# Seven-product pairs in the token mixers of a two-layer encoder on one core

## The chip, the cores and the metric

The kernel runs on one core of one Trainium2 chip. The metric is the device time of one execution in microseconds (us); the times shown are of several executions. The engines of the core have names of their own in the profile: PE is TensorE (PEld its weight loads), DVE is VectorE, ACT is ScalarE, POOL is GpSimd, SP is SyncE, which issues most of the transfers.

## The reference

Two layers work on 256 tokens of 2048 features. Each has a token mixer, a memory attention beside it that reads from the same input projection and writes through the same output projection, and a feed-forward network (FFN). All is in f32.

```python
for l in range(DEPTH):                                   # DEPTH = 2
    h = rms_norm(x, g_mix[l])
    if l % 2 == 0:                                       # layer 0: gated MLP
        tok_in, q_mem = split(h @ w_in_a, [3072])        # u and v, 1536 columns each, and 512 of q_mem
        tok_out = chunked_spatial_gating(tok_in, ...)    # gelu(u) * (w_s mixed rms_norm(gelu(v)) + b)
    else:                                                # layer 1: grouped-query attention
        tok_in, q_mem = split(h @ w_in_b, [2560])        # q 1536, k 512, v 512 columns
        tok_out = gqa_axial_attention(tok_in, ...)       # 12 query heads on 4 key heads, rotary
    mem_out = memory_attention(q_mem, mem, ...)          # 4 heads, 256 memory tokens, w_mem_kv
    x = x + concat([tok_out, mem_out]) @ w_out[l]        # 2048 x 2048
    x = x + swiglu(rms_norm(x, g_ffn[l]), w_gate_up[l], w_down[l])   # 5632 wide
```

## The kernel before

Every product keeps f32 accuracy by splitting both factors into a high part, rounded to the matmul's format, and a low part. `matmul3` (lines 196 to 200) then issues three matmuls for one product of 128x128 activations by 128x512 weights: high by high, low by high, high by low. A weight block comes from memory as a tile `raw` of 1 MB (four tiles of that kind exist); ScalarE casts it to `whi` (line 254) and VectorE subtracts to get `wlo` (line 255). Three `whi` and three `wlo` tiles exist, so weights are prepared at most some two blocks ahead of TensorE.

A projection is made in one of two forms. `Linear` (258 to 291) makes 512 output columns for both token blocks of 128: it goes through the 16 blocks of 128 input features, four to a weight tile, and issues 32 products. It prepares its weights in halves of 128x1024. It accumulates in two PSUM banks, and four such banks (`acc`) exist, so that one Linear can run while the one before is read out.

`Pair` (310 to 413) makes two groups of 512 columns in one call. It goes through eight units `i` of two feature blocks; a unit is a 2x2 block product (two token blocks, two feature blocks, two column groups) of eight products. For units listed in `fast` it uses a recursion of the Strassen kind with seven products: VectorE makes sums of weights (`T`, lines 347 to 350), and sums of activations have been made earlier (`activation_sums`, 300 to 308, from whole activations). A fast unit needs more accumulators: a Pair takes the four `acc` banks (its accumulators 2, 3, 4 and 8) and, from its first fast unit to the end of its last, also the four banks `m` (accumulators 1, 5, 6 and 7), which all transposes and attention steps use otherwise. After the last fast unit `inner` (393 to 406) reads the four `m` banks into SBUF tiles, or adds them to the residual when an `into` is given; `outer` (408 to 413) adds the `acc` banks at the end. Before, only the FFN uses Pair: gate and up together, and the down projection in two calls.

The order of the work around this is written by hand with a queue. Each Linear half-tile and each half unit of a Pair is a tick. `later(n, f)` puts f at n ticks from now: transposes of finished parts, scores, probabilities and weighted sums of the attention, residual turns, activation sums. From this order the framework makes the order of instructions on each engine, by a simulated time line with the order of the program as priority; so an engine's order is fixed before the run, and an instruction that must wait holds up what stands behind it on its engine.

Tiles of 128x512 f32 for anything short-lived come from a pool `a`: 36 of them in a mixer (`MIX_TILES`), 26 in an FFN.

In layer 0 the mixer runs three Linears for v, one for q_mem, keys and values of the memory, three for u, and four for w_out. After each u group `turn_u` (647) transposes the gated u into `cat`, the input of w_out. In layer 1 it runs k, v, three q groups (each followed by an `attend`, 461 to 525, with waits for its four steps: queries, scores, turn, weigh), q_mem, memory keys, memory values, and four for w_out. `add_residual` (586 to 597) adds a w_out result to X and queues the turn that makes the normed input of the FFN.

Of the kernel before, what the change touches and what calls it, by code (L numbers as in the profile page):

```python
# [16 lines left out]
P = 128  # L17
# [4 lines left out]
TOK = 1536  # L22
# [17 lines left out]
class Parts:  # L40


    def __init__(self):
        self.ap, self.whole = {}, {}
# [4 lines left out]
    def get(self, kc, t):  # L49
        return self.ap[kc, t]  # L50


@with_exitstack
def encoder(ctx: ExitStack, tc: tile.TileContext, x, mem, g_mix, g_ffn, w_in_a, g_v_a, w_spatial, b_spatial,
# [165 lines left out]
    def gained(tp, t, j, g, parts, keep):  # L220
# [9 lines left out]
        parts.whole[j, t] = hi, lo  # L230
# [17 lines left out]
    def halves(raw, n, step=KC4):  # L248
# [7 lines left out]
        return [(hi[:, c, :], lo[:, c, :]) for c in range(n)]  # L256

# [51 lines left out]

    class Pair:  # L310
# [28 lines left out]
        def prepare(self, i):  # L339
# [5 lines left out]
            if i in self.fast:  # L345
                T = room["p"].tile([P, KC3, NB], F32, tag="T", name=nm("T"), bufs=2)
                nc.vector.tensor_tensor(raw[:, 0], raw[:, 0], raw[:, 1], ALU.add)  # L347
                nc.vector.tensor_tensor(T[:, 0], raw[:, 0], raw[:, 3], ALU.add)
                nc.vector.tensor_tensor(T[:, 1], T[:, 0], raw[:, 1], ALU.subtract)
                nc.vector.tensor_tensor(T[:, 2], T[:, 0], raw[:, 2], ALU.add)  # L350
                self.ready[i] = raw, T

# [14 lines left out]
        def seven(self, i, raw, T):  # L367
            t1, w00, w10, w11 = halves(raw, KC4)
            t2, t3, t4 = halves(T, KC3)
# [23 lines left out]
        def inner(self):  # L393

            b, o = self.bank, self.into
            e, v, f, y = [room["p"].tile([P, NB], F32, tag=f"e{i}", name=nm("e"), bufs=1) for i in range(4)]
# [64 lines left out]
    def attend(qn, waits, keys, values, kv_of, kc0, parts):  # L461
# [42 lines left out]
        def weigh(pr):  # L504
# [12 lines left out]
            for hh in range(2):  # L517
                for t in range(NT):
                    ts = slice(t * P, (t + 1) * P)
                    parts.put(kc0 + 2 * pr + hh, t, hi[:, hh, ts], lo[:, hh, ts])  # L520
# [65 lines left out]
    def add_residual(acc, j, norm, g, parts):  # L586
# [7 lines left out]
        for t in range(NT):  # L594
            if acc:
                nc.vector.tensor_tensor(X[t][j], acc[t], X[t][j], ALU.add)
            later(1 + t, lambda t=t: turn(t))

    def residual_turns(j, norm, g, parts):
        add_residual(None, j, norm, g, parts)  # L600
# [4 lines left out]
    for l in range(DEPTH):  # L605
        scope = ExitStack()
        room["p"] = scope.enter_context(tc.tile_pool(name=f"mix{l}", bufs=MIX_TILES, reuse_waits="tile"))
        cat = Parts()
        m = Memory(l)
        if l == 0:  # L610
# [36 lines left out]
            def turn_u(us, t, c):  # L647
                tp = misc()
                transpose4(us, tp)
                hi, lo = split(v4(tp), [P, 4, P])  # L650
                for i in range(4):
# [52 lines left out]
            for c in range(3):  # L704
                acc = linear(hT, w, c * NB)
                for t in range(NT):
# [3 lines left out]
                    later(1 + t, lambda u=u, t=t, c=c: turn_u(u, t, c))  # L710
        else:
# [4 lines left out]
            acc = linear(hT, w, TOK)  # L716
            kn = head_norm(acc, norm.r, ghead["k"], True)
# [5 lines left out]
            own["v"] = scaled(linear(hT, w, TOK + MEMW), norm.r)  # L723
            for c in range(3):
                acc = linear(hT, w, c * NB)
                attend(head_norm(acc, norm.r, ghead["q"], True), (7, 8, 11, 13), lambda: own["k"], lambda: own["v"],
                       lambda h, c=c: (4 * c + h) // 3, 4 * c, cat)
            m.attend(linear(hT, w, TOK + 2 * MEMW), norm.r, cat)
            m.keys()
# [4 lines left out]
        units = kd if l else [(12, KC4), (0, KC4), (4, KC4), (8, KC4)]  # L734
        for j in range(4):
            add_residual(linear(cat, w_out[l], j * NB, units), j, norm, gslice("ffn", l), hF)
# [4 lines left out]
        room["p"] = scope.enter_context(tc.tile_pool(name=f"ffn{l}", bufs=FFN_TILES, reuse_waits="tile"))  # L741
        sums = {}
        fast = (0, 1, 2)

        def feature_sums(i):
            j, c = i // 2, 2 * (i % 2)
            whole = []
            for t in range(NT):
                hi, lo = hF.whole[j, t]
                a = big(F32, [P, 2, P])  # L750
                nc.vector.tensor_tensor(a, hi[:, c:c + 2].bitcast(F32), lo[:, c:c + 2].bitcast(F32), ALU.add)
                whole.append(a)
            sums[i] = activation_sums(*whole)
# [6 lines left out]
        for chunk in (range(0, 4), range(4, 8), range(8, 11)):  # L760
# [17 lines left out]
            for f in chunk:  # L778
                order, some = ((3, 4, 5, 0, 6, 1, 7, 2), 2) if f == 0 else ((0, 3, 1, 4, 2, 5, 6, 7), 3)
# [68 lines left out]
```

## Time and profile before

| | us |
|---|---|
| median of 3 runs | 2045.35 (2045.31 to 2046.12) |
| the profiled execution | 2045.77 |
| its span, first to last instruction | 2044.0 |
| TensorE busy in the span | 2028.7 |
| VectorE busy | 1604.7 |
| ScalarE busy | 1095.1 |

The profile is of one execution. Its span is 1.8 us shorter than its time, and its time is 0.4 us above the median. Busy times of TensorE are those of overlapping matmuls taken together; how closely matmuls follow each other is read from their start times.

### The profile page before, as it was taken

To read this page: it belongs to the slowest core of one execution; us is meant where nothing else is said; L and a number is where in the kernel's file an instruction comes from. 1 tells how busy PE (TensorE), PEld (TensorE's weight loads), DVE (VectorE), ACT (ScalarE), POOL (GpSimd) and SP (SyncE) were. 2 spreads that over 40 slices of the span, in tenths; PEclk is the share of its full clock that TensorE was granted. 3 is DMA by queue.
4 is the path that set the end of the run, shared out by engine and by line. 5 is a ranking of instruction groups with operands and counts; after the bars stand their busy time and mean duration, and the time that the engine had idled before them with its cause. 6 is when DMAs were issued, how large, how long until landed. Compare 5 with 4: busy or idle time off the path is not lost.

```text
span 2044.0 us, 24691 instructions
## 1 busy us (share of the span) xinstructions
PE 2028.7 (99%) x9298; PEld 1679.5 (82%) x9298; DVE 1604.7 (79%) x1862; ACT 1095.1 (54%) x1389; POOL 49.1 (2%) x80
## 2 busy tenths in 40 slices
PE   8999999999999999999999999999999999999999
PEld 6888888888888888888888888888888888888887
DVE  5575557998888988887666876589979899798976
ACT  7765455455444554445556665555544455444552
POOL 2010000000000000000010100000000000000000
PEclk9999999999999999999999999999999999999999
DMA  9754554655656556566556434655666555665554
GB/s 330 249 177 159 187 187 148 227 168 203 208 190 220 169 201 208 200 215 209 188 190 212 157 124 142 206 179 172 205 206 211 200 176 195 206 216 196 181 197 138
DMA packets 202432, 396.08 MB, mean 194 GB/s; under 512 B 11068, under 2 KB 11432, under 8 KB 202312
## 3 DMA queue, kind: packets, MB, share of 16 engines
q1 hardware_dynamic: 198800, 385.79, 56.4%
q0 software_dynamic: 2048, 6.42, 1.0%
q10 hardware_dynamic: 1464, 2.28, 0.3%
q8 instruction: 73, 1.20, 0.2%
q14 instruction: 47, 0.39, 0.1%
HBM read 390.26 MB, written 4.19 MB: 193 GB/s over the span
## 4 chain that ended last, share of the span: by engine, by line
PE 94%; DVE 3%; DMA 1%; issue 1%; ACT 1%; SPq 0%; DVEq 0%; ACTq 0%
PE acc L200 27%; PE acc L198 27%; PE acc L199 27%; PE m L200 4%; PE m L198 4%; PE m L199 4%; PE m L204 2%; DVE wlo L255 1%; DMA raw<-in_w_gate_up 1%; ACT whi L254 0%; PE m L500 0%; DMA x<-in_x 0%; DMA raw<-in_w_down 0%; PE m L643 0%; DVE x L413 0%
## 5 line engine op out<-in xcount | busy, mean ns | idle before, releaser
L255 DVE TENSOR_TENSOR wlo<-raw,whi 128x2048 fp32r<-128x2048 f32 (+2 forms) x465 | 836.4, 1822 | 227.0 <-ACT whi L254 224.8
L254 ACT CAST whi<-raw 128x2048 fp32r<-128x2048 f32 (+2 forms) x465 | 700.9, 1539 | 584.6 <-PE acc L199 513.3
L198 PE MATMUL acc<-whi,h 128*128 128x512 f32 x1440 | 563.6, 392 | 0.8 <-ACT whi L254 0.8
L199 PE MATMUL acc<-whi,h 128*128 128x512 f32 x1440 | 562.6, 391 | 0.0
L200 PE MATMUL acc<-wlo,h 128*128 128x512 f32 x1440 | 523.8, 392 | 1.1 <-DVE wlo L255 1.1
L198 PE MATMUL acc<-whi,a 128*128 128x512 f32 x1062 | 415.4, 392 | 0.6 <-DVE a L431 0.6
L199 PE MATMUL acc<-whi,a 128*128 128x512 f32 x1062 | 414.9, 391 | 0.0
L200 PE MATMUL acc<-wlo,a 128*128 128x512 f32 x1062 | 398.8, 391 | 0.1
L200 PEld LDWEIGHTS acc<-wlo,h 128*128 128x128 f32 x1440 | 270.6, 188 | 56.9 <-DVE wlo L255 1.9
L198 PEld LDWEIGHTS acc<-whi,h 128*128 128x128 f32 x1440 | 270.7, 188 | 55.4 <-ACT whi L254 1.2
L199 PEld LDWEIGHTS acc<-whi,h 128*128 128x128 f32 x1440 | 270.6, 188 | 55.0
L200 PEld LDWEIGHTS acc<-wlo,a 128*128 128x128 f32 x1062 | 199.7, 188 | 41.5 <-DVE wlo L255 0.5
L198 PEld LDWEIGHTS acc<-whi,a 128*128 128x128 f32 x1062 | 199.9, 188 | 41.3 <-DVE a L431 0.8
L199 PEld LDWEIGHTS acc<-whi,a 128*128 128x128 f32 x1062 | 199.9, 188 | 40.5
L254 ACT CAST whi<-T 128x1536 fp32r<-128x1536 f32 x82 | 121.4, 1481 | 143.3 <-PE acc L199 104.1
L255 DVE TENSOR_TENSOR wlo<-T,whi 128x1536 fp32r<-128x1536 f32 x82 | 143.5, 1750 | 38.8 <-ACT whi L254 38.8
L198 PE MATMUL m<-whi,a 128*128 128x512 f32 x264 | 104.2, 395 | 0.7 <-ACT whi L254 0.7
L199 PE MATMUL m<-whi,a 128*128 128x512 f32 x264 | 102.8, 390 | 0.0
L347 DVE TENSOR_TENSOR raw<-raw 128x512 f32<-128x512 f32 x82 | 56.1, 684 | 56.4 <-DMA raw<-in_w_gate_up 54.3
L200 PE MATMUL m<-wlo,a 128*128 128x512 f32 x264 | 89.6, 389 | 0.0
L192 ACT CAST a<-m 128x512 fp32r<-128x512 f32 x80 | 46.3, 586 | 50.7 <-PE m L204 32.6
L193 DVE TENSOR_TENSOR a<-m,a 128x512 fp32r<-128x512 f32 x80 | 54.0, 683 | 17.5 <-ACT a L192 17.5
(126 smaller groups left out, 1469.0 us busy)
## 6 DMA issues: line engine op xcount, KB each, us to landing
raw<-in_w_gate_up SPq DMA_DIRECT2D x352, 512.0 KB, 4.7
raw<-in_w_down SPq DMA_DIRECT2D x176, 512.0 KB, 5.2
raw<-in_w_out SPq DMA_DIRECT2D x32, 1024.0 KB, 5.1
raw<-in_w_in_a SPq DMA_DIRECT2D x24, 1024.0 KB, 5.3
raw<-in_w_in_b SPq DMA_DIRECT2D x24, 1024.0 KB, 5.2
raw<-in_w_mem_kv SPq DMA_DIRECT2D x16, 1024.0 KB, 5.2
raw<-in_w_in_a SPq DMA_DIRECT2D x7, 512.0 KB, 6.1
x<-in_x SPq DMA_DIRECT2D x8, 256.0 KB, 5.7
```

Of the source, the lines that this page charges most:

```text
L192: nc.scalar.copy(hi, src)
L193: nc.vector.tensor_tensor(lo, src, hi.bitcast(F32), ALU.subtract)
L198: nc.tensor.matmul(out, lhsT=a[0], rhs=b[0], start=start, stop=False)
L199: nc.tensor.matmul(out, lhsT=a[1], rhs=b[0], start=False, stop=False)
L200: nc.tensor.matmul(out, lhsT=a[0], rhs=b[1], start=False, stop=stop)
L204: nc.tensor.transpose(dst[:, c * P:(c + 1) * P], src[:, c * P:(c + 1) * P], ident)
L254: nc.scalar.copy(hi[:, cut], raw[:, cut])
L255: nc.vector.tensor_tensor(lo[:, cut], raw[:, cut], hi[:, cut].bitcast(F32), ALU.subtract)
L347: nc.vector.tensor_tensor(raw[:, 0], raw[:, 0], raw[:, 1], ALU.add)
```

## The change

Twelve Linears become six Pairs. In layer 0 the first two u groups are one Pair with three fast units of eight; in layer 1 keys and values are one Pair with two; w_out of each layer is two Pairs with two fast units each, which add into X. The third u group, v, all q groups and the memory projections stay Linears. For the fast units `pair_sums` makes activation sums of `hT` (as `mix_sums`) and of `cat` (as `cat_sums`, used by both Pairs of a w_out). In a mixer a fast unit takes its T from three tiles of the pool `a` instead of one of 128x1536, and `halves_of` casts and subtracts them one by one. `inner` takes its four tiles from `a` there as well. The residual turns of two groups are queued after each w_out Pair. The order of units in the first FFN Pair changes, and in layer 1 the turns and weighted sums of the second and third query group are queued one and two ticks later.

```diff
@@ Parts, gained, split
+    def put_pair(self, i, t, hi, lo):
+        self.two[i, t] = hi, lo
...
+    def halves_of(blocks):
+        hi = wp.tile([P, KC4, NB], F32R, tag="whi", name=nm("whi"))
+        lo = wp.tile([P, KC4, NB], F32R, tag="wlo", name=nm("wlo"))
+        for c, b in enumerate(blocks):
+            nc.scalar.copy(hi[:, c], b)
+            nc.vector.tensor_tensor(lo[:, c], b, hi[:, c].bitcast(F32), ALU.subtract)
+        return [(hi[:, c, :], lo[:, c, :]) for c in range(len(blocks))]
...
+    def pair_sums(parts, i):
+        whole = []
+        for t in range(NT):
+            hi, lo = parts.two[i, t]
+            a = big(F32, [P, 2, P])
+            nc.vector.tensor_tensor(a, hi.bitcast(F32), lo.bitcast(F32), ALU.add)
+            whole.append(a)
+        return activation_sums(*whole)
@@ Pair.prepare
-                T = room["p"].tile([P, KC3, NB], F32, tag="T", name=nm("T"), bufs=2)
+                if room["T"]:
+                    T = room["p"].tile([P, KC3, NB], F32, tag="T", name=nm("T"), bufs=2)
+                    T = [T, *(T[:, c] for c in range(KC3))]
+                else:
+                    T = [None, *(big() for _ in range(KC3))]
@@ add_residual
-    def add_residual(acc, j, norm, g, parts):
+    def add_residual(wait, j, norm, g, parts):
...
         for t in range(NT):
-            if acc:
-                nc.vector.tensor_tensor(X[t][j], acc[t], X[t][j], ALU.add)
-            later(1 + t, lambda t=t: turn(t))
+            later(wait + 1 + t, lambda t=t: turn(t))
@@ layer 0
-            for c in range(3):
-                acc = linear(hT, w, c * NB)
+            def gated(acc, c, wait):
                 for t in range(NT):
...
+            for i in range(3):
+                later(1 + 2 * i, lambda i=i: mix_sum(i))
+            g = Pair(hT, mix_sums, w, 0, NB, (3, 4, 0, 5, 1, 6, 2, 7), (0, 1, 2))
+            g.run()
+            for c in range(2):
+                gated([g.out[t][c] for t in range(NT)], c, 1 + 2 * c)
+            for i in range(2):
+                later(5 + 2 * i, lambda i=i: cat_sum(i))
+            gated(linear(hT, w, 2 * NB), 2, 1)
@@ layer 1
-            acc = linear(hT, w, TOK)
-            kn = head_norm(acc, norm.r, ghead["k"], True)
+            for i in range(2):
+                later(2 + 2 * i, lambda i=i: mix_sum(i))
+            g = Pair(hT, mix_sums, w, TOK, TOK + MEMW, (2, 3, 4, 0, 5, 1, 6, 7), (0, 1))
+            g.run()
+            kn = head_norm([g.out[t][0] for t in range(NT)], norm.r, ghead["k"], True)
...
-            own["v"] = scaled(linear(hT, w, TOK + MEMW), norm.r)
+            own["v"] = scaled([g.out[t][1] for t in range(NT)], norm.r)
...
-                attend(head_norm(acc, norm.r, ghead["q"], True), (7, 8, 11, 13), lambda: own["k"], lambda: own["v"],
+                attend(head_norm(acc, norm.r, ghead["q"], True), (7, 8, 11 + c, 13 + c), lambda: own["k"], lambda: own["v"],
...
+            for i in range(2):
+                later(2 + 8 * i, lambda i=i: cat_sum(i))
             m.keys()
             m.values()
@@ w_out
-        units = kd if l else [(12, KC4), (0, KC4), (4, KC4), (8, KC4)]
-        for j in range(4):
-            add_residual(linear(cat, w_out[l], j * NB, units), j, norm, gslice("ffn", l), hF)
+        orders = ((2, 3, 0, 4, 1, 5, 6, 7), (2, 3, 0, 4, 1, 5, 6, 7)) if l else \
+            ((6, 0, 7, 1, 3, 2, 4, 5), (6, 7, 0, 3, 1, 2, 4, 5))
+        pairs = []
+        for jj in range(2):
+            into = [[X[t][2 * jj + n] for n in range(2)] for t in range(NT)]
+            fast = (0, 1)
+            pairs.append(Pair(cat, cat_sums, w_out[l], 2 * jj * NB, (2 * jj + 1) * NB, orders[jj], fast, into))
+        for jj, g in enumerate(pairs):
+            g.run(None if jj else pairs[1])
+            for n in range(2):
+                add_residual(2 * n, 2 * jj + n, norm, gslice("ffn", l), hF)
@@ FFN, first Pair
-                order, some = ((3, 4, 5, 0, 6, 1, 7, 2), 2) if f == 0 else ((0, 3, 1, 4, 2, 5, 6, 7), 3)
+                order, some = ((2, 3, 4, 0, 5, 1, 6, 7), 2) if f == 0 else ((0, 3, 1, 4, 2, 5, 6, 7), 3)
```

49 lines of the change are left out of this document (26 added, 23 removed).

## The prediction

> **What bounds the kernel now.** I read the page first: busy shares, slices, the chain that ended last.
>
> ```profile
> span 2044.0 us, 24691 instructions
> PE 2028.7 (99%) x9298; PEld 1679.5 (82%) x9298; DVE 1604.7 (79%) x1862; ACT 1095.1 (54%) x1389; POOL 49.1 (2%) x80
> ...
> PE   8999999999999999999999999999999999999999
> ...
> DVE  5575557998888988887666876589979899798976
> ...
> PE 94%; DVE 3%; DMA 1%; issue 1%; ACT 1%; SPq 0%; DVEq 0%; ACTq 0%
> ```
>
> TensorE is busy almost everywhere and carries 94% of the chain; it is idle for 2044.0 - 2028.7 = 15.3 us in all. VectorE has room in the mixers (slices of 5 to 7) and little in the FFNs (8 and 9). Since busy matmuls overlap, I next took a gap-free stretch of the timeline of TensorE. Columns are start, duration, engine, line.
>
> ```profile
> 1263.24 0.40 PE L198 MATMUL acc<-whi,a 128*128 128x512 f32 x1
> ...
> 1277.33 0.39 PE L200 MATMUL acc<-wlo,a 128*128 128x512 f32 x1
> ```
>
> These are the first and the last of 63 matmuls in a row: 14.09 / 62 = 0.2273 us from start to start. Where TensorE never waits, that is the price of one. The windows then show where it waits (stretch, length, busy time and count for PE, PEld, DVE, ACT, POOL, then clock, DMA share, GB/s).
>
> ```profile
> 0.00:20.00 20.00, 14.43 (x65) 10.90 (x66) 10.76 (x24) 16.39 (x52) 2.42 (x10) 1.00 0.89 301
> 340.00:360.00 20.00, 18.86 (x83) 15.27 (x82) 16.76 (x20) 11.68 (x10) 0.00 (x0) 1.00 0.40 129
> 360.00:380.00 20.00, 19.69 (x85) 15.61 (x84) 20.00 (x22) 9.92 (x8) 0.00 (x0) 1.00 0.61 206
> 1200.00:1220.00 20.00, 16.79 (x88) 14.14 (x87) 13.02 (x35) 11.91 (x40) 1.83 (x2) 0.91 0.31 105
> 406.00:448.00 42.00, 42.00 (x191) 34.79 (x190) 38.01 (x40) 23.14 (x20) 0.00 (x0) 1.00 0.57 190
> ```
>
> Idle are 5.6 us at the start, which the change doesn't touch, 1.4 at the start of the first FFN, and 3.2 near 1206 in the mixer of layer 1. The last row is one FFN Pair with three fast units: VectorE busy for 38.0 of 42 us (90%), TensorE never idle. So a Pair with that load on VectorE runs without gaps.
>
> **The products.** A fast unit has seven products for eight, so it saves three matmuls. Fast units in mixers: 3 (u) + 2 (keys and values) + 4 Pairs of w_out x 2 = 13; the first FFN Pair keeps its two. 13 x 3 = 39 matmuls, and 39 x 0.2273 = **8.9 us**. Transposes and attention matmuls stay as many.
>
> The Trainium skill (Perfetto Trace Analysis, Identifying the Most-Contended Engine) says that matmul busy time is no measure of how near TensorE is to its limit, and that the busy share of its weight loads is one. By that this TensorE has 18% of headroom, and the 39 would be worth 0.82 x 8.9 = 7.3 us. The page here has weight loads at 82%, but in the gap-free FFN Pair above they are at 34.79 of 42, or 83%, so that share is already full; I keep 8.9, and the other figure lies inside my range.
>
> **What VectorE gets.** Rows by form (count, then busy us and mean ns):
>
> ```profile
> L255 DVE TENSOR_TENSOR wlo<-raw,whi 128x2048 fp32r<-128x2048 f32 x264 | 599.4, 2285 | 105.7 <-ACT whi L254 104.9
> L255 DVE TENSOR_TENSOR wlo<-raw,whi 128x1024 fp32r<-128x1024 f32 x199 | 235.6, 1220 | 119.2 <-ACT whi L254 117.9 <-PE m L204 0.7
> L255 DVE TENSOR_TENSOR wlo<-raw,whi 128x512 fp32r<-128x512 f32 x2 | 1.4, 692 | 2.0 <-ACT whi L254 2.0
> L348 DVE TENSOR_TENSOR T<-raw 128x512 f32<-128x512 f32 x82 | 56.0, 683 | 0.5
> L398 DVE TENSOR_TENSOR e<-m,e 128x512 f32<-128x512 f32 x32 | 21.8, 682 | 0.0
> L193 DVE TENSOR_TENSOR a<-a,a 128x512 fp32r<-128x512 f32 x15 | 10.2, 681 | 0.0
> L751 DVE TENSOR_TENSOR a<-h,h 128x256 f32<-128x256 f32 x12 | 4.5, 416 | 0.0
> L303 DVE TENSOR_TENSOR a<-a 128x128 f32<-128x128 f32 x15 | 4.2, 281 | 0.0
> L596 DVE TENSOR_TENSOR x<-acc,x 128x512 f32<-128x512 f32 x16 | 11.1, 692 | 15.3 <-PE acc L200 15.2
> L431 DVE SCALAR_TENSOR_TENSOR a<-acc,s,a 128x128 f32<-128x128 f32 x64 | 17.6, 342 | 0.0
> ```
>
> A fast unit adds four weight sums and three separate subtractions: 4 x 0.683 + 3 x 0.692 = 4.8 us. One activation sum costs 2 x 0.416 + 4 x 0.281 + 0.681 = 2.6 us; there are nine. `inner` is 4 x 0.682 = 2.7 us, adding into X as much again, and so is `outer`, which in w_out takes the place of as many additions (L596, 0.692). A weight tile in one piece saves 2 x 1.220 - 2.285 = 0.15 us. Whether that has cover is seen by stage:
>
> ```profile
> 114.00:139.00 25.00, 25.00 (x140) 21.64 (x139) 18.11 (x31) 14.56 (x39) 3.17 (x5) 1.00 0.44 140
> 139.00:162.00 23.00, 23.00 (x120) 19.47 (x119) 16.48 (x35) 13.93 (x28) 1.06 (x1) 1.00 0.52 180
> 162.00:184.00 22.00, 22.00 (x117) 18.72 (x116) 13.87 (x18) 11.88 (x17) 0.00 (x0) 1.00 0.45 144
> 184.00:207.00 23.00, 23.00 (x107) 19.05 (x106) 12.03 (x12) 10.46 (x12) 0.00 (x0) 1.00 0.54 183
> ...
> 230.00:252.50 22.50, 22.50 (x105) 18.64 (x104) 12.03 (x12) 10.32 (x12) 0.00 (x0) 1.00 0.55 188
> 252.50:275.00 22.50, 22.50 (x105) 18.64 (x104) 13.27 (x18) 12.41 (x24) 0.00 (x0) 1.00 0.55 188
> 275.00:298.00 23.00, 23.00 (x107) 19.02 (x107) 13.30 (x19) 12.36 (x24) 0.00 (x0) 1.00 0.55 183
> 298.00:320.50 22.50, 22.50 (x105) 18.64 (x104) 13.60 (x17) 12.16 (x22) 0.00 (x0) 1.00 0.54 179
> ...
> 1030.00:1052.00 22.00, 22.00 (x106) 18.31 (x105) 14.84 (x27) 14.45 (x34) 3.10 (x6) 1.00 0.57 187
> 1052.00:1074.00 22.00, 22.00 (x100) 18.22 (x100) 15.85 (x27) 12.12 (x26) 3.52 (x5) 1.00 0.68 218
> ```
>
> - w_out of layer 0 (230 to 320.5): VectorE 52.2 of 90.5 us. After: 52.2 - 16 x 0.15 + 4 x 4.8 + 2 x 2.7 + 2 x 2.7 = 79.8, on 90.5 - 12 x 0.227 = 87.8 us of TensorE: 91%, the load of the FFN Pair. Cost nothing; without that cover, each us that VectorE lacks is one of TensorE.
> - The u Pair (162 to 207): 25.9 of 45 becomes 25.9 - 8 x 0.15 + 3 x 4.8 + 2.7 + 2.7 + 3 x 2.6 = 52.3 on 43.0 us. Over by 9.3. Of that `outer` (2.7) falls after the last product, and two weight tiles (4.6) can be ready when the Pair begins, which leaves 2.0 us of idle TensorE.
> - Keys and values (1030 to 1074): 30.7 of 44 becomes 30.7 - 1.2 + 2 x 4.8 + 2.7 + 2.7 + 2 x 2.6 = 49.7 on 42.6. Over by 7.1; but again `outer` falls behind, and so does the norm of the keys (8 x 0.342 = 2.7 and its rotary steps), so about 0 is left.
>
> From below these two starts cost nothing, from above 9.3 + 7.1 = 16.4 us, if no tile is ready ahead. I take 2.0 and, for an order fixed ahead that doesn't quite fit, as much as the first FFN start shows (1.14 + 0.31): **+3.5**. At the two FFN starts the turns of two column groups come together, where one came before. That is eight more gain operations (0.34 as L431, nearest by size) and two more additions, 4.1 us of VectorE each, in front of the same three units of eight products; bounds -1.4 to +8.2 for both, taken as 0, since the first fast unit comes fourth there as before.
>
> ScalarE gets 39 casts for T, nothing longer than what VectorE does with them, at a share of 54%. PSUM: the four `m` banks are taken from the first to the last fast unit; by the lists of units the transposes and weighted sums due in a Pair come before that stretch, so I cost it at nothing; a read-out that is late would hold TensorE for about one subtraction, 0.68 us, at each of six Pairs. From a Linear to a Pair the last two `acc` banks must be read within half a unit, 12 x 0.227 = 2.7 us; two reads of the size of L596 take 1.4, so that costs nothing either while VectorE is on time. The transfers carry the same bytes in halves of 512 KB; their shares of time stay near 0.55. For SyncE's queue that is 48 more issues. What holds that queue is shown by its waits (us in total, times, longest):
>
> ```profile
> SPq L357 <- DVE wlo L255: 1037.5, 247, 11.6
> ```
>
> It stands waiting for VectorE to release a `raw` tile for half of the span, so its own time is covered; a late subtraction delays the next transfer too, which is part of the 16.4 above.
>
> **The later turns.** The gap near 1206:
>
> ```profile
> 1205.67 0.28 PE L200 MATMUL m<-a,a 128*128 128x256 f32 x1
> 1208.58 0.63 PE L500 MATMUL m<-ident,a 128*128 128x128 f32 x4 [2.63 <-DVE a L490]
> 1209.79 0.79 PE L198 MATMUL acc<-whi,a 128*128 128x512 f32 x1 [0.58 <-DVE a L431]
> ...
> 1213.22 0.39 PE L200 MATMUL acc<-wlo,a 128*128 128x512 f32 x1
> ```
>
> ```profile
> 1183.28 0.36 DVE L427 TENSOR_SCALAR s<-s,s 128x4 f32<-128x4 f32 x2 [0.73 <-POOL s L185]
> ...
> 1208.61 2.15 DVE L431 SCALAR_TENSOR_TENSOR a<-acc,s,a 128x128 f32<-128x128 f32 x8
> ```
>
> Transposes of probabilities (L500) stand first in TensorE's queue and wait 2.8 us for the softmax; then the memory values wait 0.8 for a bank; then eight matmuls take 3.43 us instead of 1.82, at a lower clock. Together 5.2 us. The turn moves back by two ticks of 12 matmuls (5.4 us), so its wait could go. But next in line is the bank: the values need the accumulators of q_mem, and L431, which reads those, came at 1208.61, though its factor was there at 1183.28. It lacked room: by my count the pool `a` then holds 16 memory tiles, 4 of own values, 2 of keys, 8 of `cat`, 1 of gains and 4 of turned queries, 35 of 36. The change adds an activation sum there (5 tiles while made, 2 kept). So the gap may go (-5.2) or come twice (+5.2). I take **-1.5**: its first wait shortens, its second stays. Behind a waiting transpose stands all of TensorE.
>
> **Sum.** -8.9 + 3.5 - 1.5 = -6.9 us. The profiled execution took 2045.77 (span 2044.0 and 1.8 around it), 0.4 above the median; from the median, 2045.35 - 6.9 = **2038.5 us**.
>
> **Rivals.** (1) As forecast, 2038.5: for it the FFN Pair without gaps; chance 0.50. (2) No new gap, and the old one goes: -8.9 - 5.2, **2031.3**. For it that most stretches have no idle time; against it the crowded starts; 0.18. (3) The pool `a` in layer 1 is the bound: the sums take tiles, q_mem's accumulators are held for longer, the gap comes twice: -8.9 + 3.5 + 5.2 = -0.2, **2045.2**, no change. For it the 25 us that L431 waited; 0.20. (4) Slower: VectorE becomes the bound at the starts of the u Pair and the key-value Pair, because the sums stand in its queue ahead of the weights and no tile is ready: +16.4 - 8.9 = +7.5, **2052.9**. It beats the gain from 8.9 us of new idle time on. For it 122% of load on paper; against it the FFN, and the slack of VectorE in the stage before (the first two rows of the stages, memory keys and values: 18.11 of 25 and 16.48 of 23 us, 72%); 0.12. That fewer matmuls are not issued can't be: the lists fix their number.
>
> **How the numbers follow.** This kernel's measurement tells 0.2% (4.1 us) from no change. Faster by that (under 2041.3): nearly all of (1), all of (2), 0.66. Within: (3) and a little of (1), 0.22. Slower (over 2049.4): (4), 0.12. The range runs from (2) to past (3), 2031 to 2047, and leaves out (4) and the outer ends.
>
> **What would show it.** Right: 39 fewer matmuls, idle time of TensorE of 14 to 20 us, idle pieces at the start of the u Pair, VectorE near 90% in w_out. Wrong: idle time over 24 us, or TensorE waiting for `wlo` through a whole Pair (4), or a gap of over 5 us beside memory keys or values (3). Under 13 us means (2).

## The result and the profile after

The changed kernel is slower: 2060.84 us median of four runs (2058.98 to 2062.43) beside 2045.73 (2045.31 to 2046.52) of the kernel before on the same chip, a ratio of 1.0074 with a 95% interval of 1.0062 to 1.0086. The forecast of 2038.5 us missed, by the sign too; the time lies outside the forecast range (2031 to 2047) and above the slowest rival (2052.9). The changed code is five lines further down: the weight cast and subtraction are L259 and L260, the matmuls L202 to L204, transposes L208, the norm of heads L460, the turns of probabilities L529. The page of the profiled execution (2058.98 us):

```profile
span 2057.2 us, 24904 instructions
PE 2028.7 (99%) x9259; PEld 1675.0 (81%) x9259; DVE 1700.2 (83%) x2016; ACT 1119.0 (54%) x1395; POOL 57.0 (3%) x80
...
DVE  5578889998889988887588877899979899798976
...
PE 92%; DVE 5%; ACT 1%; issue 1%; DMA 0%; SPq 0%; DVEq 0%; ACTq 0%
```

There are 39 matmuls fewer, as counted. TensorE is idle for 2057.2 - 2028.7 = 28.5 us, 13.2 more than before, just what the span gained, and over the 24 us that the prediction named as a sign of being wrong. That its busy time did not fall by 8.9 us is no contradiction: a matmul behind a long wait can take longer (0.63 us instead of 0.39 near 1217), and short waits vanish inside overlapping ones. So the busy total hid the loss, and the length of each stage shows it. The table takes the time from the first 128x512 product of a stage on TensorE's timeline to that of the next; "expected" is the saved products at 0.2273 us, and in the w_out and FFN rows the eight transposes (0.7 us; four in a row without a wait take 0.35 us from the first start to the next matmul's) of one column group that are now turned in the FFN's start instead of in w_out.

```
stage                               before   after    change   expected   lost
u (layer 0)                          71.96    77.72    +5.8      -2.0      7.8
w_out, layer 0                       90.82    89.43    -1.4      -3.4      2.0
FFN 0, first four gate-up Pairs     172.86   175.47    +2.6      +0.7      1.9
keys and values, q groups, q_mem    146.39   145.21    -1.2      -1.4      0.2
memory keys, values, w_out, layer 1 160.85   164.38    +3.5      -3.4      6.9
FFN 1, first four gate-up Pairs     171.43   175.56    +4.1      +0.7      3.4
```

The waits of TensorE (what waits, releaser: us in total, times, longest) name where:

```profile
PE m L529 <- DVE a L519: 4.4, 4, 1.3
...
PE m L208 <- DVE a L460: 3.2, 1, 3.2
PE m L202 <- ACT whi L268: 3.1, 1, 3.1
PE acc L202 <- ACT whi L259: 1.9, 3, 1.1
PE m L204 <- DVE wlo L260: 1.7, 2, 0.9
...
PE acc L202 <- DVE a L442: 1.4, 1, 1.4
PE acc L202 <- ACT a L744: 1.1, 1, 1.1
```

They are the softmax, the norm of heads, the cast of a sum of weights in the u Pair (L268), weights at the FFN starts, and two banks that are not yet read out. The windows of the stages shown before, in the same columns:

```profile
162.00:184.00 22.00, 22.00 (x118) 18.74 (x117) 19.93 (x36) 10.59 (x17) 0.00 (x0) 1.00 0.30 96
184.00:207.00 23.00, 18.82 (x76) 14.82 (x75) 18.51 (x27) 14.17 (x17) 0.00 (x0) 0.93 0.40 137
...
262.00:284.00 22.00, 22.00 (x100) 18.23 (x100) 19.10 (x19) 9.06 (x9) 0.00 (x0) 1.00 0.76 241
...
306.00:326.00 20.00, 20.00 (x90) 16.55 (x89) 20.00 (x20) 11.18 (x11) 0.00 (x0) 1.00 0.76 263
...
1200.00:1220.00 20.00, 16.84 (x89) 14.28 (x88) 13.98 (x34) 12.39 (x38) 1.83 (x2) 0.91 0.44 145
1250.00:1270.00 20.00, 15.64 (x87) 13.16 (x86) 14.50 (x34) 10.25 (x30) 0.00 (x0) 0.91 0.09 27
```

In the two windows of w_out Pairs (262 to 284, 306 to 326) TensorE has no gap, with VectorE at 87 and 100%. The loss lies in the seams: inside the u Pair, at 1211 (the old gap near 1206), and at 1255, where there was none. In the u Pair, the timeline of VectorE (start, duration, line; idle before in brackets) shows why:

```profile
186.24 0.75 DVE L330 TENSOR_TENSOR a<-h,h 128x256 f32<-128x256 f32 x2
187.02 0.29 DVE L317 TENSOR_TENSOR a<-a 128x128 f32<-128x128 f32 x1
...
188.78 0.69 DVE L197 TENSOR_TENSOR a<-a,a 128x512 fp32r<-128x512 f32 x1 [0.74 <-ACT a L196]
189.39 0.69 DVE L376 TENSOR_TENSOR a<-raw 128x512 f32<-128x512 f32 x1
190.11 0.69 DVE L377 TENSOR_TENSOR a<-a,raw 128x512 f32<-128x512 f32 x1
```

The activation sums of a later unit (L330, L317 to L320, L197) stand ahead of the weight sums (L376 to L378) that the next products need. TensorE started its last ready matmul at 187.37 and the next one, on the first of these sums, at 190.86.

### The profile page after: what moved, and what is told of

Read it like the earlier page. It is cut to its first block, busy times and chain, and to the rows that moved or that the text cites. A ratio compares the mean times of both kernels' runs of the same rounds, so it can differ in the third digit from the quotient of the medians.

```text
span 2057.2 us, 24904 instructions
## 1 busy us (share of the span) xinstructions
PE 2028.7 (99%) x9259; PEld 1675.0 (81%) x9259; DVE 1700.2 (83%) x2016; ACT 1119.0 (54%) x1395; POOL 57.0 (3%) x80
## 4 chain that ended last, share of the span: by engine, by line
PE 92%; DVE 5%; ACT 1%; issue 1%; DMA 0%; SPq 0%; DVEq 0%; ACTq 0%
PE acc L204 26%; PE acc L202 25%; PE acc L203 25%; PE m L204 4%; PE m L202 4%; PE m L203 4%; DVE wlo L260 2%; PE m L208 2%; ACT whi L259 1%; DVE a L197 0%; ACT a L514 0%; PE m L529 0%; DMA raw<-in_w_out 0%; PE m L678 0%; DVE x L442 0%
## 5 line engine op out<-in xcount | busy, mean ns | idle before, releaser
L259 ACT CAST whi<-raw 128x2048 fp32r<-128x2048 f32 (+2 forms) x417 | 695.8, 1694 | 582.1 <-PE acc L203 520.4
L260 DVE TENSOR_TENSOR wlo<-raw,whi 128x2048 fp32r<-128x2048 f32 (+2 forms) x417 | 833.3, 2017 | 172.6 <-ACT whi L259 171.4
L202 PE MATMUL acc<-whi,h 128*128 128x512 f32 x1410 | 552.9, 393 | 3.4 <-ACT whi L259 1.9
L203 PE MATMUL acc<-whi,h 128*128 128x512 f32 x1410 | 552.0, 391 | 0.0
L204 PE MATMUL acc<-wlo,h 128*128 128x512 f32 x1410 | 509.8, 392 | 0.4 <-DVE wlo L260 0.4
L202 PE MATMUL acc<-whi,a 128*128 128x512 f32 x1027 | 403.3, 393 | 1.1 <-ACT a L744 1.1
L203 PE MATMUL acc<-whi,a 128*128 128x512 f32 x1027 | 401.2, 391 | 0.0
L204 PE MATMUL acc<-wlo,a 128*128 128x512 f32 x1027 | 378.0, 391 | 0.2 <-DVE wlo L260 0.2
L202 PEld LDWEIGHTS acc<-whi,h 128*128 128x128 f32 x1410 | 265.7, 188 | 58.6 <-ACT whi L259 5.1
L204 PEld LDWEIGHTS acc<-wlo,h 128*128 128x128 f32 x1410 | 265.1, 188 | 55.8 <-DVE wlo L260 1.6
L203 PEld LDWEIGHTS acc<-whi,h 128*128 128x128 f32 x1410 | 265.6, 188 | 53.9
L204 PEld LDWEIGHTS acc<-wlo,a 128*128 128x128 f32 x1027 | 193.4, 188 | 41.6 <-DVE wlo L260 1.4
L202 PEld LDWEIGHTS acc<-whi,a 128*128 128x128 f32 x1027 | 193.6, 188 | 40.8 <-ACT a L744 1.6
L203 PEld LDWEIGHTS acc<-whi,a 128*128 128x128 f32 x1027 | 193.6, 188 | 39.2
L259 ACT CAST whi<-T 128x1536 fp32r<-128x1536 f32 x82 | 121.4, 1480 | 132.7 <-PE acc L203 95.1
L260 DVE TENSOR_TENSOR wlo<-T,whi 128x1536 fp32r<-128x1536 f32 x82 | 143.8, 1754 | 37.7 <-ACT whi L259 37.7
L202 PE MATMUL m<-whi,a 128*128 128x512 f32 x311 | 122.8, 395 | 3.8 <-ACT whi L268 3.1
L203 PE MATMUL m<-whi,a 128*128 128x512 f32 x311 | 121.2, 390 | 0.0
L375 DVE TENSOR_TENSOR raw<-raw 128x512 f32<-128x512 f32 x95 | 65.3, 687 | 58.7 <-DMA raw<-in_w_gate_up 47.8
L204 PE MATMUL m<-wlo,a 128*128 128x512 f32 x311 | 107.6, 390 | 1.7 <-DVE wlo L260 1.7
L202 PEld LDWEIGHTS m<-whi,a 128*128 128x128 f32 x311 | 58.4, 188 | 19.5 <-ACT whi L259 4.6
L204 PEld LDWEIGHTS m<-wlo,a 128*128 128x128 f32 x311 | 58.4, 188 | 14.7 <-DVE wlo L260 2.6
```

What stands on the lines that cost most here:

```text
L202: nc.tensor.matmul(out, lhsT=a[0], rhs=b[0], start=start, stop=False)
L203: nc.tensor.matmul(out, lhsT=a[1], rhs=b[0], start=False, stop=False)
L204: nc.tensor.matmul(out, lhsT=a[0], rhs=b[1], start=False, stop=stop)
L259: nc.scalar.copy(hi[:, cut], raw[:, cut])
L260: nc.vector.tensor_tensor(lo[:, cut], raw[:, cut], hi[:, cut].bitcast(F32), ALU.subtract)
```

## The experiments

All parts of the change sit behind constants in a copy of the changed kernel: `U_PAIR`, `KV_PAIR` and `OUT_PAIRS` choose Pair or the Linears of before, `LATER` the later turns (1 or 0), `FIRST` the unit order of the first FFN Pair. Lines are five further than in the changed kernel (L207 for L202), in the kernels with a staggered Pair twelve more. Medians are in us; the ratio is to before on the same chip, with its 95% interval.

```
only_u       2052.05  1.0036 [1.0024, 1.0049]   out_first    2044.14  0.9998 [0.9988, 1.0007]
only_kv      2044.27  0.9996 [0.9986, 1.0005]   out_stagger  2044.17  0.9994 [0.9984, 1.0004]
only_out     2048.86  1.0020 [1.0010, 1.0030]   all_parts    2048.63  1.0019 [1.0009, 1.0028]
only_turns   2045.49  1.0003 [0.9993, 1.0012]   qn_room      2039.84  0.9974 [0.9964, 0.9985]
u_early      2045.95  1.0005 [0.9995, 1.0015]   before_room  2040.20  0.9978 [0.9969, 0.9987]
u_stagger    2045.95  1.0003 [0.9994, 1.0013]   room_out     2042.47  0.9990 [0.9980, 0.9999]
out_late     2049.94  1.0024 [1.0014, 1.0033]   room_all     2044.58  0.9998 [0.9989, 1.0008]
out_room     2047.90  1.0014 [1.0005, 1.0024]   room_qTV     2042.33  0.9987 [0.9978, 0.9997]
room_t18     2053.32  1.0041 [1.0026, 1.0056]   room_qTV_u   2045.31  1.0000 [0.9991, 1.0010]
```

### One part at a time

`only_u`: the u Pair alone, the rest as before. The other three of this part differ from it by these constants only.

```diff
-KV_PAIR = True
-OUT_PAIRS = True
-LATER = 1
-FIRST = (2, 3, 4, 0, 5, 1, 6, 7)
+KV_PAIR = False
+OUT_PAIRS = False
+LATER = 0
+FIRST = (3, 4, 5, 0, 6, 1, 7, 2)
```

> The u Pair of layer 0 alone, the rest as before. Theory 1 (the loss of the u stage is made there: activation sums and T stand in VectorE's queue in front of weights, and the two hand-overs wait): the u stage takes 77.7 us where it took 72.0, so the kernel is some 5.8 us slower than before, about 2051.5 us, with a gap of about 3 us after the second fast unit begins and the lower clock behind it. Rival (the u stage suffers from the w_out Pairs behind it, whose T and sums are prepared in its last part): the stage is shorter than before by 9 x 0.227 = 2 us, about 2043.7 us. Layer 1 unchanged by both.

The u stage took 78.3 us and TensorE waited 3.1 us for the first weight sum at the same place: the loss of the u Pair is its own.

`only_kv`: `KV_PAIR = True` alone.

> Keys and values of layer 1 as one Pair alone. Theory 1: the stage had no loss after the change (145.2 us where 146.4 were), so -6 x 0.227 = -1.4 us, 2044.4 us, and the gap near 1206 stays at its 5 us. Rival (the Pair shifts the attention behind it and makes the two gaps of layer 1): 6 us of gaps more beside the memory keys and values, about 2050 us.

Its stage became 1.2 us shorter, nearly the six products. No loss.

`only_out`: `OUT_PAIRS = True` with the new `FIRST`.

> The four w_out Pairs alone, with the new order of the first FFN Pair, turns as before. Theory 2 (the two gaps of layer 1 come from the activation sums of w_out, which take tiles of the pool while the attention needs them): -24 x 0.227 = -5.5, +6 in the memory keys and values, +2 in w_out of layer 0, +5 at the two FFN starts: about +7.5, 2053 us. Rival (the gaps come from the later turns): without the 6, about +1.5, 2047 us, with the gap near 1206 as before.

w_out of layer 0 came out 3.5 us shorter, all that was expected. But the FFN starts grew by 2.6 and 3.9 us, and near 1250 TensorE lost 3.4 us around the softmax of the memory attention (4.8 us in which only sixteen transposes ran), where it had lost none. The 2.0 us lost in w_out of layer 0 in the full change come from its neighbour: with Linears for u it took 87.3 us in every run with w_out Pairs, with the u Pair 88.8 to 89.4.

`only_turns`: `LATER = 1` alone.

> Only the later turns and weighted sums of the second and third query group. Theory 2: the gap near 1206 stays or shrinks by its first wait, -2.8 to 0 us, 2043 to 2045.7 us. Rival (the later turns make the two gaps of layer 1): a second gap of some 6 us near 1255, about 2052 us.

```profile
PE m L213 <- DVE a L465: 3.1, 1, 3.1
```

The gap near 1206 stayed; only its releaser changed, from the softmax to the norm of the memory queries. The later turns gain nothing.

### Mending the u Pair and the FFN starts

`u_early`: `only_u` with the sums made during the three Linears before.

```diff
+            for i, n in enumerate((3, 12, 20)):
+                later(n, lambda i=i: mix_sum(i))
             m.attend(linear(hT, w, 2 * TOK), norm.r, cat)
...
-                for i in range(3):
-                    later(1 + 2 * i, lambda i=i: mix_sum(i))
```

> The u Pair alone (as in only_u), with its three activation sums made earlier: in the q_mem, the memory keys and the memory values, 3, 12 and 20 ticks after the last v group. Theory 1 (order in VectorE's queue: sums stand ahead of the weights of the second fast unit): the gap of 3.1 + 0.6 us near 190 and the low clock behind it go, the wait of 1.4 us where the third u group takes over the banks stays; u stage about 72 to 73 us, kernel about 2046 us. Rival (VectorE is short of time over the whole stage, whatever its order): gaps of about the same sum elsewhere in the stage, 2050 to 2052 us.

The wait for L273 is gone, and the u stage takes 73.7 us instead of 78.3. Twelve score matmuls of 128x256 have moved into it from the stage of the memory values, which became 1.5 us shorter (24.15 instead of 25.61). So the two stages are compared together: 97.8 us, after 103.9 in `only_u` and 97.6 with Linears. The sums where they stood were the cause. Whether it was their place or their load isn't separated, since the run also takes them out of the stage (VectorE busy for 58.7 us there, after 64.2); in `only_u` VectorE was busy for 64.2 of 78.3 us, so over the stage it had time left. But 1.8 us of waits came near 166, where the memory attention's softmax and its values' read-out now are late at the start of the Pair, and so the Pair still gains nothing over Linears.

`u_stagger`: `u_early`, with the first two units of the Pair interleaved by token block, so that accumulators 4 and 8 are wanted twelve matmuls later.

```diff
+            if stagger:
...
+                for t in range(NT):
+                    for i in first:
+                        self.eight(i, None, cut[i], (t,))
```

> As u_early, with the same interleaving of the first two units of the u Pair. Theory 3: the 1.7 us lost near 166, where the Pair takes over the banks of the memory values of layer 0, go; u stage and what lies before it end at 229.5 to 230 instead of 231.4, 2044.2 us. Rival: no change, 2046 us.

No difference: the waits near 166 stay.

`out_first`: `only_out` with the unit order of before.

```diff
-FIRST = (2, 3, 4, 0, 5, 1, 6, 7)
+FIRST = (3, 4, 5, 0, 6, 1, 7, 2)
```

> The w_out Pairs alone, with the unit order of the first FFN Pair as it was in the kernel before. Theory 4 (the new order, with its first fast unit's weights no later but the turns nearer, makes the FFN starts longer): the first FFN chunks come back from 175.4 and 175.4 us to some 173.5 and 172.2, 2044 us. Rival (the turns and additions of two column groups together in front of the first Pair make it): no change, about 2049 us.

The first four Pairs of the two FFNs took 172.65 and 171.90 us, after 175.42 and 175.35: the new order cost 2.8 and 3.5 us. The same stretch in `only_out` and in `out_first` (windows, columns as above):

```profile
341.50:361.50 20.00, 18.52 (x80) 14.34 (x79) 18.37 (x25) 11.45 (x10) 0.00 (x0) 1.00 0.51 175
```

```profile
341.50:361.50 20.00, 20.00 (x90) 16.29 (x88) 18.11 (x15) 10.62 (x8) 0.00 (x0) 1.00 0.62 218
```

Ten more matmuls in the same 20 us at the same load of VectorE: again the order, not the amount. Both orders have unit 0 fourth and unit 1 sixth, so the position of the fast units is not the reason. Which dependence makes the waits was not isolated.

### The gap near 1206 and the one near 1250

`qn_room`: the kernel before, with one change in layer 1: the two normed tiles of the memory queries come from the pool of the normed features (16 tiles, free again by then) instead of pool `a`.

```diff
-            qn = big()
+            qn = keep(F32, [P, NB]) if keep else big()
```

> The kernel before, but the two tiles of normed memory queries of layer 1 come from the pool of normed features, which is free by then. Theory 5 (room: near 1206 the read-out of q_mem's banks waits for two tiles of the mixer's pool, and the memory values wait for those banks): the read-out comes some 20 us earlier, the gap of 3.7 us idle and 1.6 us of low clock goes, 2040 us. Rival (it stands late in VectorE's order for another reason, or the wait for the softmax alone makes the gap): 2045 us, the gap at 2.6 to 3.2 us.

```profile
1181.92 0.36 DVE L461 TENSOR_SCALAR s<-s,s 128x4 f32<-128x4 f32 x2 [0.71 <-POOL s L194]
1182.19 1.38 DVE L465 SCALAR_TENSOR_TENSOR h<-acc,s,a 128x128 f32<-128x128 f32 x5
```

```profile
1200.00:1220.00 20.00, 20.00 (x114) 17.22 (x112) 14.09 (x28) 15.64 (x43) 1.92 (x2) 1.00 0.40 142
```

The norm follows its factor at once, where before it came 25 us later, and TensorE has no idle time between 1200 and 1220. The stage is 5.0 us shorter. At 2039.84 us this is the fastest version run; it beats both kernels, and only the place of two tiles differs from the kernel before. `before_room` does the same for the memory keys too:

> The kernel before, with the normed memory queries and the normed memory keys of layer 1 (two tiles each) in the pool of the normed features instead of pool `a`. Theory (the room in `a` also holds up the norm of the memory keys, but without Pairs that norm is early enough once the queries are out of the pool): as with the queries alone, 2039 to 2040.5 us, no gap over 1 us between 1195 and 1260. Rival (the keys' norm is late only by VectorE's queue): the same time, so this run tells apart only whether the keys' tiles cost anything of themselves; a time under 2038.5 would say that they were late without Pairs too.

It is as fast, and the keys' norm starts 0.27 us after its factor, so the keys' tiles are not late without Pairs.

`out_late`: `only_out` with the memory attention of layer 1 due later, (4, 17, 19, 21), and one more slow unit ahead in its first w_out Pair.

```diff
-            attend(head_norm(acc, r, ghead[f"mq{self.l}"]), (4, 13, 17, 19), lambda: self.kT, lambda: self.V, lambda h: h,
+            attend(head_norm(acc, r, ghead[f"mq{self.l}"]), (4, 17, 19, 21) if self.l else (4, 13, 17, 19), lambda: self.kT, lambda: self.V, lambda h: h,
...
-        orders = ((2, 3, 0, 4, 1, 5, 6, 7), (2, 3, 0, 4, 1, 5, 6, 7)) if l else \
+        orders = ((2, 3, 4, 0, 5, 1, 6, 7), (2, 3, 0, 4, 1, 5, 6, 7)) if l else \
```

> The w_out Pairs alone (as in only_out); in layer 1 the steps of the memory attention after the queries come 4, 2 and 2 ticks later, and three units of eight products stand ahead of the first fast one. Theory 3 (hand-over: the Pair takes all four accumulator banks, the second half of its first unit needs those of the memory values, and their read-out on ScalarE and VectorE stands behind the softmax): the read-out comes first, the gap of 3.4 us idle near 1250 goes, 2044.5 to 2046 us. Rival (room: tiles of the pool run short because of the activation sums): a gap of that size stays, about 2049 us.

The gap near 1250 went, as theory 3 has it, but the time is the rival's: waits of 0.9 and 0.7 us for weights came near 1266, and one of 2.0 us for the banks of the first Pair at 1289. The run changes the due times and the unit order at once, so which of them made these waits isn't shown. `out_room`: `only_out`, with the sums of `cat` out of pool `a` (`split` gets the pool as an argument):

```diff
-            cat_sums[i] = pair_sums(cat, i)
+            cat_sums[i] = pair_sums(cat, i, kept if l else None)
```

> The w_out Pairs alone; the high and low parts of the activation sums of w_out in layer 1 are put in the pool of normed features, where there is room, so that four tiles of the mixer's pool are free. Theory 3: nothing changes near 1250, about 2048.9 us. Rival (room): the gap near 1250 goes and the one near 1206 gets no longer than in the kernel before, about 2045 us.

Both gaps stayed. `out_stagger`: `out_first` with the first two units of layer 1's first w_out Pair interleaved as in `u_stagger`:

> As out_first (w_out Pairs alone, old unit order in the FFN), and in layer 1 the first w_out Pair does the first token block of its first two units before the second block of either, so that the banks of the memory values are needed 24 instead of 12 products' matmuls later (2.7 us). Theory 3 (hand-over of the banks): the 3.4 us idle near 1250 shrink by 2.7 or go, 2041 to 2042 us. Rival (TensorE waits there for the softmax, whatever it has beside it): no change, 2044 us.

No change of the gap: the extra products ran before the scores and not beside the softmax.

`all_parts`: all Pairs, early sums, old `FIRST`, `LATER = 0`, both staggers, and the memory queries as in `qn_room`.

> All Pairs of the change, with early sums for u, the old unit order in the FFN, no later turns, interleaved first units after the memory values in both layers, and the memory queries in the other pool. If the theories hold together: 8.9 us of matmuls, the gap near 1206 (5.2) and at most 3 us of hand-over: 2045 - 14 + 3 = 2034 us. If gaps only move from one place to the next: 2040 to 2046 us.

It came out 14.6 us above the first sum, and 2.6 us above the range for gaps that only move. The queries' norm was on time, but the wait moved to the norm of the memory keys, 27 us after its factor:

```profile
1207.26 0.36 DVE L473 TENSOR_SCALAR s<-s,mem_r 128x4 f32<-128x4 f32 x2 [0.99 <-POOL s L194]
...
1234.36 2.15 DVE L477 SCALAR_TENSOR_TENSOR a<-acc,s,a 128x128 f32<-128x128 f32 x8
```

`room_out`: key-value Pair and w_out Pairs, u as Linears, old `FIRST`, no later turns; queries, keys and the sums of `cat` out of pool `a`. `room_all` adds the u Pair with early sums.

```diff
-            kn = head_norm(acc, self.r, ghead[f"mk{self.l}"])
+            kn = head_norm(acc, self.r, ghead[f"mk{self.l}"], False, kept if self.l else None)
```

> Key-value Pair and w_out Pairs, the first FFN order of before, u in three Linears, and in layer 1 the normed memory queries, the normed memory keys and the activation sums of `cat` out of pool `a`. Theory (room in `a` made the memory attention late, first at the queries' norm near 1206, then at the keys' norm, then at the softmax near 1250): the gaps near 1206 and 1232 go and those near 1250 shrink to under 1.5 us in all; from before 5.2 (gap) + 5.4 (two more Pairs in w_out of layer 0) + 5.4 (layer 1) + 1.4 to 2.7 (keys and values) less 1 to 3 at the starts: 2031 to 2035 us. Rival (the softmax near 1250 stands there because a Pair needs its banks earlier than a Linear, whatever room there is): 4 us of waits for the softmax stay, 2036 to 2039 us.

> The same with the u Pair of layer 0, whose activation sums are made during the Linears before it. Theory: room_out less what the u Pair gains with early sums, which by itself was -1.4 to +0.7 us: 2030 to 2036 us. Rival (the u Pair pushes layer 0's gelu into the start of w_out, 1 us of wait there): 2035 to 2039 us, slower than room_out.

Both were slower than either theory allowed. The gap near 1206 went, but the softmax still stood in the open (four waits, 3.8 us), as the rival said. VectorE and ScalarE of `room_out`:

```profile
1204.07 0.36 DVE L461 TENSOR_SCALAR s<-s,mem_r 128x4 f32<-128x4 f32 x2 [0.99 <-POOL s L194]
...
1223.12 0.68 DVE L202 TENSOR_TENSOR h<-a,h 128x512 fp32r<-128x512 f32 x1
1223.72 1.63 DVE L465 SCALAR_TENSOR_TENSOR h<-acc,s,a 128x128 f32<-128x128 f32 x6
```

```profile
1245.04 0.47 ACT L519 ACTIVATE a<-m,s 128x256 f32<-128x256 f32 x1
...
1245.48 1.26 ACT L568 ACTIVATE a<-acc,mem_r 128x512 fp32r<-128x512 f32 x2
```

The keys' norm came 20 us after its factor, right behind the write of a `cat` sum that now asks for a tile of the same pool first. And L568, which reads the memory values out of their banks, stood behind the whole softmax, though TensorE's last 128x512 products before it were at 1235.8. `room_qTV` has the sums of `cat` in `a` again, and queries (normed and turned), keys and values of the memory out of it.

```diff
-            st["qT"] = heads_T(qn)
+            st["qT"] = heads_T(qn, keep)
...
-            self.V = scaled(linear(self.parts, w_mem_kv[self.l], NB), self.r)
+            self.V = scaled(linear(self.parts, w_mem_kv[self.l], NB), self.r, kept if self.l else None)
```

> As room_out (key-value Pair, w_out Pairs, u in Linears), but `cat`'s activation sums are back in pool `a`, and in layer 1 the memory queries (normed and turned), the normed memory keys and the memory values are in the pool of the normed features. In room_out the memory values were read out of their banks (10 us after their last product) behind the whole softmax, and no product was left for TensorE meanwhile. Theory (that read-out waited for room in pool `a`, and so kept the two banks from the w_out Pair): the read-out now comes before the softmax, 18 products of w_out (18 x 0.227 = 4.1 us) run while the softmax does, and of the 8 us lost between 1236 and 1250 in room_out 2 to 4 are left: 2036.5 to 2039.5 us. Rival (the Pair needs the softmax before it has products to run, whatever the room): 8 us stay lost there, 2041 to 2043 us.

```profile
PE m L213 <- DVE h L465: 3.4, 1, 3.4
...
PE m L534 <- DVE a L524: 0.8, 1, 0.8
```

```profile
1230.78 1.27 ACT L568 ACTIVATE h<-acc,mem_r 128x512 fp32r<-128x512 f32 x2
```

The theory held for the softmax: the values are read at 1230.78, 14.6 us ahead of the softmax, 18 matmuls run beside it (the expectation calls them products; they are six products of three), and its waits fall from 3.8 to 0.8 us. But the keys' norm is the gap again, 3.4 us at 1233, now behind the turned queries in the same pool, and the total stayed at 2042.33: the waits are the theory's, the time is the rival's. `room_t18`: the same with turns and weighing one tick later, (4, 13, 18, 20).

> room_qTV with the turns of the memory probabilities and the weighing of the values one tick later in layer 1 (18 and 20). Theory: the turns still stand right behind the 18 products, so they wait as in room_qTV, but the weighing is split and gives up some waits for splits of probabilities: within 1 us of room_qTV. Rival (the time left near 1240 comes from the due times, not from banks): over 2 us less than room_qTV.

Both were wrong: 11 us slower. The waits at 1233 and 1252 are those of `room_qTV`; new is above all one of 4.2 us, the second w_out Pair waiting for the first one's banks (L447), with slower weights ahead of it. `room_qTV_u`: with the u Pair.

> room_qTV with the u Pair and its early sums as well: all the Pairs of the change, with the old first FFN order and without the later turns. Theory (layer 0's part is unchanged: the u Pair came out +0.9 with w_out as Linears and, against room_out, +2.1 in room_all): room_qTV plus 1 to 2.5 us, 2038 to 2041.5 us. Rival (the u Pair pays once layer 1 is free of waits): at or under room_qTV.

The ratio is 1.0000, 3.0 us above `room_qTV`, where the theory gave 1 to 2.5: the u Pair does not pay here either.

## Why the prediction was wrong, step by step

- **Products: right.** 39 fewer, and each worth about the whole 0.2273 us where nothing else broke: `only_kv` shortened its stage by 1.2 us (1.4 expected), and `only_out` w_out of layer 0 by 3.5 (3.4). The headroom reading of the Trainium skill (Perfetto Trace Analysis, Identifying the Most-Contended Engine), by which they would be worth 82% of that, isn't borne out by `only_out`: with it, w_out would be 2.9 us shorter, not 3.5.
- **"w_out of layer 0: cost nothing": right by itself** (`only_out`). In the full change 2.0 us were lost there, 1.1 of them in the wait for a gelu that the u stage left to w_out's start.
- **Start of the u Pair, +2.0 and 1.4 for an order that doesn't fit: mis-sized; it was 7.8.** The beginning of the Pair did run without a gap (162 to 184), so "two weight tiles can be ready" isn't what failed. The balance of VectorE's load over the whole stage is: in the middle of the Pair its queue had activation sums ahead of the weight sums, and TensorE waited 3.1 us there. Rival (4) had that mechanism, at the beginning of the Pair. `u_early` took the sums away from there and, counted over this stage and the one before, 6.1 us with them; 2.3 us of loss stayed, about as much as the waits near 166 (1.8) and 207 (0.7).
- **Start of the key-value Pair, about 0: right** (0.2). Rival (4) fails there.
- **FFN starts "taken as 0, since the first fast unit comes fourth there as before": failed.** They lost 5.3 us within the bounds given (-1.4 to +8.2). The fast units do stand where they stood, but the slow ones between them do not, and `out_first` shows that this order costs 6.2 us.
- **Banks "costs nothing while VectorE is on time": failed at the condition.** ScalarE and VectorE were late: 1.4 us at 211.15 (L442) and 1.1 us at 240.56 (gelu, L744), and in the 1255 gap.
- **Later turns, -1.5: failed.** "Its first wait shortens, its second stays" described a gap whose waits share one cause. The norm stood at 1208.61 for lack of a tile, as the step itself counted (35 of 36), and without the softmax wait TensorE simply waited for that norm. `only_turns` gained nothing and `qn_room` all 5 us.
- **Layer 1 as a whole:** the forecast -1.5 plus products; measured 6.9 us over the products. Rival (3) named the pool as the bound and a second gap as its price, and that is nearest. What it missed is the place: not the same wait twice, but the softmax of the memory attention. Before, 28 matmuls of a Linear (6.4 us) stood between the last scores and the first turn; a Pair wants all four banks, two of which the memory values still held.

By their ratios, the four parts alone add up to 7.4 - 0.8 + 4.1 + 0.6 = 11 us of the 15; the rest comes from their meeting, in layer 1 and at the start of w_out. My chances gave "slower" 0.12. I had priced each seam by the load of its stage; the waits came from what stood in front of an operand on an engine or in a pool. At the FFN starts (`out_first`) and at 1206 (`qn_room`) a single edit shows that; in the u Pair order and load are not separated.

Still open is why the keys' norm is late in `all_parts` and `room_qTV`. That tiles of one pool are handed out in the order in which the program asks for them, so that a free tile waits behind an earlier request, fits `room_out` and `room_qTV` (the norm came right behind the write of the tile asked for before it) and `before_room`, but was argued, not isolated. A pool of more than 36 tiles wasn't tried.

No version with Pairs in the mixers beat `qn_room`. One that looks better wasn't run: `qn_room` with only the key-value Pair and the w_out Pairs of layer 0. In `out_first` the w_out of layer 0 was 3.5 us shorter and the FFN start behind it no longer than before, and in `only_kv` the stage of keys and values was 1.2 us shorter. An estimate from these is 2039.8 - 3.5 - 1.2 = 2035 us, if no gap moves as in `room_out`.

## What to carry to other kernels

Where TensorE is busy 99% of the time, fewer products gain only what the seams let through: list, for each new seam, which instructions stand in front of the first product's operands on each engine, and not only the load of the stage. Before a gap is mended by moving what waits in it, look for a ready operation that ran late (a factor at 1183, its use at 1208): here two tiles from another pool gained 5.5 us, where the change that removed 39 matmuls lost 15. And test the parts of a change singly, since a neutral and a losing edit can hide a gain.

## What the runs showed of the hardware

A wait can cost more than its length. After one of 3.3 us, the starts of 128x512 matmuls were 0.43 us apart instead of 0.23, for some 3 us; the timeline and the windows of the changed kernel:

```profile
1215.80 0.40 PE L204 MATMUL acc<-wlo,a 128*128 128x512 f32 x1
1216.04 0.54 PE L202 MATMUL acc<-whi,a 128*128 128x512 f32 x1
1216.38 0.63 PE L203 MATMUL acc<-whi,a 128*128 128x512 f32 x1
...
1219.37 0.48 PE L204 MATMUL acc<-wlo,a 128*128 128x512 f32 x1
```

```profile
211.00:216.00 5.00, 3.60 (x17) 2.68 (x16) 5.00 (x7) 4.00 (x4) 0.00 (x0) 1.00 0.89 281
...
1215.00:1220.00 5.00, 5.00 (x16) 3.89 (x17) 4.24 (x16) 1.21 (x5) 0.62 (x1) 0.66 0.45 160
1260.00:1265.00 5.00, 4.19 (x17) 3.24 (x15) 4.63 (x10) 3.40 (x8) 0.00 (x0) 0.66 0.00 0
```

TensorE started again at 1214.49, ran 1.9 us at about full speed, and then for 3.0 us at half: seven matmuls, 0.2 us extra each. After a single wait of 1.4 us (211 to 216) the clock stayed at 1.00; after four waits in a row of 0.8 to 1.3 us (1255 to 1261) it fell to 0.66. In all this makes the 3.3 us gap worth some 4.7. The Trainium skill (TensorE: Matmul & The Clock Gate, Part 1: The HAM clock gate) has the clock halved after an idle window of about 3.4 us. The two slow stretches above are about that long (0.66 over 5 us is half speed for 3.4 us), but the waits ahead of them were shorter, 3.3 us or four pieces with transposes between. In `room_out` the slow stretch was longer: 0.53 over 1243 to 1250 is half speed for 6.6 us.

Nor does the length of a wait decide alone. The kernel before waited 2.63 and 0.58 us near 1206, and its clock over the next 5 us was 0.66; `only_kv` waited as long in the same place and stayed at 1.00:

```profile
1206.55 0.63 PE L534 MATMUL m<-ident,a 128*128 128x128 f32 x4 [2.63 <-DVE a L524]
1207.76 0.50 PE L207 MATMUL acc<-whi,a 128*128 128x512 f32 x1 [0.58 <-DVE a L465]
```

```profile
1206.00:1211.00 5.00, 3.87 (x18) 3.09 (x19) 4.64 (x19) 2.22 (x10) 1.84 (x2) 1.00 0.61 210
```

In this one execution the stretch from the memory keys to w_out was 1.4 us shorter for it, which is no gain of the key-value Pair. What else decides isn't shown.
